# Scan steps of a gated encoder layer: masks in one instruction, the state's split at a step's beginning, an addition on GpSimd, and a gate's SiLU made in the attention

## The chip, the core and the metric

The kernel runs on one core of a Trainium2 chip. The time is the device time of one execution in microseconds, the median of three runs. The engines are TensorE (PE in the rows; PEld is its loading of weights), VectorE (DVE), ScalarE (ACT), GpSimd (POOL) and SyncE (SP), which only issues DMAs here.

## The reference

One encoder layer is applied to two sequences, of 512 and of 1024 tokens, each with a condition vector of its own; the width is 1024.

```python
h = rms_norm(x, norm_g) * (1 + scale) + shift          # shift, scale, gate from silu(c) @ w_ada + b_ada
proj = h @ w_in
(q_c, kv_c, k_rope, gate_a, z, xbc, dt_f_raw, dt_b_raw, g_a, g_b) = split(proj)
attn = mla_attention(q, k, v)                          # 8 heads; q, k, v from q_c, kv_c, k_rope
branch_a = (attn * silu(gate_a)) @ w_proj_a
xbc = silu(dwconv_centred(xbc, conv_w, conv_b))        # 5 taps
xs, B, C = split(xbc)
y = bidirectional_ssd(xs, dt_f, dt_b, A_f, A_b, B, C, d_f, d_b)
y = rms_norm(y * silu(z)) ; branch_b = y @ w_proj_b    # norm in 4 groups
out = x + gate * ((sigmoid(g_a) * branch_a + sigmoid(g_b) * branch_b) @ w_out)
```

The scan (`bidirectional_ssd`) works in chunks of 128 tokens, in 4 groups of 8 heads of 64 channels, with 128 state dimensions. In one direction, for a chunk with running sums `a` of the decays:

```python
CB     = C @ B.T                                       # 128 x 128, one for all heads of a group
y_diag = (CB * exp(where(tri, a_l - a_s, -inf))) @ (x * dt)
y_off  = (C @ state) * exp(a)                          # the part carried from other chunks
state  = state * exp(a_last) + B.T @ (exp(a_last - a) * dt * x)
```

The backward direction is the same on the reversed sequence, with the other triangle for a mask.

## The kernel before

All 1536 tokens are worked on in three windows of 512. A float32 product that has to be exact is made of three TensorE products (`mm3`, L88 to L90): a high part `h` (a rounded copy) and a low part `l` (the rest) of each factor. ACT makes the copy (L226 for weights, "wh<-ws"), DVE the rest (L85, "wl<-ws,wh").

The stages in order of time, in microseconds of the profile: a prologue (0 to 85); then four groups, each with its convolution blocks, its scan and its z gate; the attention (1598 to 2190); the final projections (2190 to 2714). The scans lie in the windows 219 to 386, 570 to 735, 937 to 1100 and 1330 to 1500.

**A scan.** `prepass` goes backwards through a sequence's chunks, makes the backward states and writes them to DRAM (sbD). `mainpass` goes forwards. The work of a chunk is cut into two units of four heads (`us`). For a chunk there are:

- `head` (L635): transposed blocks `xb` of x and B (for the first chunk of a sequence by `tok`, L588 to L592, on TensorE and ACT, otherwise loaded, L644), the product of B and C (L651, into PSUM "sm"), and its two masked copies `cu` (L653 and L654, DVE);
- `state` (L683): ACT copies (L688, L690) and GpSimd's subtractions (L689 "btl", L691 "zt") split the weighted x and B for the `mm3` of `follow` (L88 to L90 "sm<-zt,..."), after which DVE makes the new state (L607, L609 "stf");
- `decays` (L657): loads of the decays into `eb` (L663);
- `carried` (L667): an exponential on ACT (L672), the product of C and the carried state on TensorE (L677, into "sm"), its scaling (L678), and where both directions are there the sum of the two (L680, DVE).

And for a unit: `distances` (two loads `ab`, L706), `weights` (two subtractions on GpSimd, L714; eight scaled copies of `cu` on ACT, L718 and L719, and their sum on DVE, L720; a selection on DVE, L721; an exponential on ACT, L722), `weigh` (L727, DVE) and `products` (L738, TensorE, into PSUM "py"). `tail` (L743, L744, DVE) adds both parts up. PSUM has three slots "sm", which the transposes, the mask product, the state's product and the carried products use in turn.

Between a scan's steps `feed` puts pieces of other projections of the input, the fillers, at 0.66 of a piece for a step. One kind, "gate", is gate_a: from PSUM, ACT makes tanh of its half (L524), DVE makes (tanh + 1) times the gate (L525), and SP writes the result to DRAM (sgA, L526).

**The attention** works in 24 units (sequence, head, window). For each there is a list of work on the scores (`scores`: transposes, and four blocks with maxima and exponentials, L1025) and a list on the values (`values`). `merge` puts lists together in proportion, so that each entry's place depends on its list's length. The scores are one unit or more ahead of the values. `gates` makes the reciprocal sums `rb`, loads gate_a's part `gt` (L1042) and multiplies the two on GpSimd (L1043); at the end of a unit DVE multiplies the output by it and by 0.5 (L1072).

**Order.** Each engine works through a queue of its own in an order that is fixed when the program is built: a scheduler takes, by the order of the program and by what is ready in its own model, the next instruction for each engine. So where a line stands in the program moves instructions on every engine. Buffers (`bufs`) are used in turn; a second use waits for the last reader of the first.

Of the kernel before, what the change touches and what calls it, by code (L numbers as in the profile page):

```python
# [65 lines left out]
def _body(nc, tc, A, O):  # L66
# [447 lines left out]
    def filler(kind, i):  # L514
# [6 lines left out]
        elif kind == "gate":  # L521
            def ev(w, ps):
                t = tmp("ft")
                S.activation(t, ps, AF.Tanh, scale=0.5)  # L524
                V.scalar_tensor_tensor(t, t, 1.0, ps, op0=ALU.add, op1=ALU.mult)  # L525
                nc.sync.dma_start(out=sgA[i][w], in_=t)  # L526
            return inproj_steps(BLK_GATE + i, ev)
        else:
            dst = tga if kind == "ga" else tgb

            def ev(w, ps):
                t = tmp("ft")
                S.activation(t, ps, AF.Tanh, scale=0.5)
                nc.sync.dma_start(out=dst[i][w], in_=t)
            return inproj_steps((BLK_GA if kind == "ga" else BLK_GB) + i, ev)
# [34 lines left out]
    for g in range(G):  # L570
# [61 lines left out]
        def mainpass(o, n):  # L632
# [5 lines left out]
            def head(c):  # L638
# [8 lines left out]
                if c < c1 - 1:  # L647
                    sb = pS.tile([P, W], F32, name="sb", bufs=2)
                    nc.sync.dma_start(out=sb, in_=sbD[g][c])
                pc = smp.tile([P, P], F32, name="sm")  # L650
                PE.matmul(pc, lhsT=Bt[:, cs_], rhs=Ct[:, cs_], start=True, stop=True)  # L651
                cu = pS.tile([P, 2, P], F32, name="cu", bufs=2)
                V.tensor_tensor(cu[:, 0, :], pc, triF, op=ALU.mult)  # L653
                V.tensor_tensor(cu[:, 1, :], pc, triB, op=ALU.mult)  # L654
                stt[c] = dict(xt=xt, bt=bt, sb=sb, cu=cu)
# [11 lines left out]
            def carried(c):  # L667
# [11 lines left out]
                if len(eb) == 2:  # L679
                    V.tensor_tensor(eb[1], eb[1], eb[0], op=ALU.add)  # L680
# [66 lines left out]
            us = [(c, u) for c in range(c0, c1) for u in range(nu)]  # L747
            head(c0)
# [7 lines left out]
            for i in range(len(us) + 1):  # L756
                if i < len(us):
                    weigh(*us[i])
# [4 lines left out]
                if i < len(us) and us[i][1] == 1:  # L763
                    follow(us[i][0])
                    carried(us[i][0])
# [4 lines left out]
                if i < len(us) and us[i][1] == 0:  # L770
                    c = us[i][0]
                    state(c)
# [198 lines left out]
    def scores(u):  # L971
# [55 lines left out]

        def gates():
# [12 lines left out]
            gt = p2.tile([P, W], F32, name="gt", bufs=1)  # L1041
            nc.sync.dma_start(out=gt, in_=sgA[hd][o // W + w])  # L1042
# [4 lines left out]
        return [turn_n, turn_r], [lambda b=b: block(b) for b in range(4)]  # L1047
# [220 lines left out]
```

## Time and profile before

| | us |
|---|---|
| median of 3 runs | 2715.68 (2711.13 to 2715.99) |
| profiled execution, device time | 2716.42 |
| its span in the trace | 2714.4 |
| TensorE busy | 2586.5 (95%) |
| VectorE busy | 1833.5 (68%) |
| ScalarE busy | 1322.6 (49%) |
| GpSimd busy | 505.1 (19%) |

The mean granted clock of TensorE in the profiled execution was 0.985 of full speed. Busy time is a sum over stages with different limits; the shares of single stages, the waits of TensorE and single stretches in order of time are in the rows below. In a timeline row stand the start, the length, the engine, the line, the operation, the tiles "out<-in", the shape and, in brackets, how long the engine had been idle before it and what ended that.

### The profile page before, as it was taken

How to read it: one execution, taken by the hardware profiler on the slowest of the kernel's cores; microseconds unless marked ns; L12 is line 12 of the kernel's file. 1: busy time of each engine (PE TensorE's matmuls, PEld its weight loads, DVE VectorE, ACT ScalarE, POOL GpSimd, SP SyncE). 2: the span in 40 equal slices, each digit the busy share in tenths (PEclk: the TensorE clock that was granted, in tenths of full speed). 3: DMA queues.
4: the chain of work that ended last, by engine and by line, in shares of the span. 5: the costliest groups of instructions: out<-in, count | busy, mean ns of one | idle time of the engine just before them, and what ended most of it. 6: DMA issues, size and time to landing. Idle time of an engine off the chain costs nothing. (4 is left out here: it accounts for less than half of the span.)

```text
span 2714.4 us, 36314 instructions
## 1 busy us (share of the span) xinstructions
PE 2586.5 (95%) x12810; PEld 2080.5 (77%) x12810; DVE 1833.5 (68%) x2962; ACT 1322.6 (49%) x2954; POOL 505.1 (19%) x455
## 2 busy tenths in 40 slices
PE   6999999999999998999998999999999999999999
PEld 2776777877778766878766888888888788888887
DVE  5878785788946678557777568877777753466631
ACT  5545654456624456564556357666665651111210
POOL 1013440023400035110135024322222200000000
PEclk8999999999999999999999999999999999999999
DMA  7227662156722266542466322211110252255433
GB/s 249 77 78 208 187 168 94 39 179 187 207 62 86 82 208 183 136 147 74 146 191 188 92 96 87 84 44 43 34 40 28 71 186 70 78 156 163 128 125 101
DMA packets 211205, 325.86 MB, mean 120 GB/s; under 512 B 24816, under 2 KB 74064, under 8 KB 210256
## 3 DMA queue, kind: packets, MB, share of 16 engines
q1 hardware_dynamic: 211024, 323.55, 39.9%
q8 instruction: 101, 1.65, 0.3%
q14 instruction: 80, 0.66, 0.1%
HBM read 245.56 MB, written 77.91 MB: 119 GB/s over the span
## 5 line engine op out<-in xcount | busy, mean ns | idle before, releaser
L88 PE MATMUL mm<-hH,wh 128*128 128x512 f32 x1656 | 670.2, 405 | 2.3 <-ACT hH L218 2.0
L89 PE MATMUL mm<-hL,wh 128*128 128x512 f32 x1656 | 662.0, 400 | 3.6 <-DVE hL L219 3.6
L90 PE MATMUL mm<-hH,wl 128*128 128x512 f32 x1656 | 653.7, 395 | 1.3 <-DVE wl L85 1.2
L88 PEld LDWEIGHTS mm<-hH,wh 128*128 128x128 f32 x1656 | 314.6, 190 | 84.6 <-issue 14.6
L89 PEld LDWEIGHTS mm<-hL,wh 128*128 128x128 f32 x1656 | 315.4, 190 | 77.3 <-issue 10.2
L90 PEld LDWEIGHTS mm<-hH,wl 128*128 128x128 f32 x1656 | 314.6, 190 | 73.2 <-issue 6.1
L714 POOL TENSOR_TENSOR ab<-ab,dg 128x512 f32<-128x512 f32 x192 | 236.9, 1246 | 418.5 <-DMA ab<-arD 293.4
L88 PE MATMUL mm<-hi,wh 128*128 128x512 f32 x768 | 298.8, 389 | 0.0
L90 PE MATMUL mm<-hi,wl 128*128 128x512 f32 x768 | 298.8, 389 | 0.0
L89 PE MATMUL mm<-lo,wh 128*128 128x512 f32 x768 | 298.8, 389 | 0.0
L85 DVE TENSOR_TENSOR wl<-ws,wh 128x512 fp32r<-128x512 f32 x210 | 151.3, 722 | 134.4 <-ACT wh L226 86.7
L361 ACT CAST wh<-ws 128x512 fp32r<-128x512 f32 x72 | 44.9, 623 | 326.4 <-PE mm L89 311.3
L88 PEld LDWEIGHTS mm<-hi,wh 128*128 128x128 f32 x768 | 144.1, 188 | 30.1
L89 PEld LDWEIGHTS mm<-lo,wh 128*128 128x128 f32 x768 | 144.1, 188 | 29.9
L90 PEld LDWEIGHTS mm<-hi,wl 128*128 128x128 f32 x768 | 144.1, 188 | 29.9
L719 ACT ACTIVATE wt<-cu,dg 128x128 f32<-128x128 f32 x384 | 141.3, 391 | 46.5 <-DVE cu L653 46.1
L1025 ACT ACTIVATE pp<-sp,smx,rq 128x512 f32<-128x512 f32 x160 | 123.6, 777 | 54.9 <-DVE smx L1020 38.8
L361 ACT CAST ph<-tp 128x512 fp32r<-128x512 f32 x160 | 95.3, 598 | 110.4 <-PE tp L1059 110.2
L689 POOL TENSOR_TENSOR btl<-xb,bth 128x128 fp32r<-128x128 f32 x40 | 28.5, 713 | 607.5 <-ACT bth L688 607.4
L563 DVE SCALAR_TENSOR_TENSOR xs<-raw,cwh,xs 128x511 f32<-128x511 f32 (+3 forms) x128 | 129.7, 1021 | 17.5 <-ACT xs L559 14.8
L718 ACT ACTIVATE t<-cu,dg 128x128 f32<-128x128 f32 x384 | 137.3, 390 | 2.6 <-DVE cu L654 2.4
L721 DVE COPY_PREDICATED ab<-maskb,ab 128x512 f32<-128x512 uint8 x96 | 86.4, 905 | 69.3 <-POOL ab L714 69.3
(293 smaller groups left out, 5018.5 us busy)
## 6 DMA issues: line engine op xcount, KB each, us to landing
ab<-arD SPq DMA_DIRECT2D x192, 256.0 KB
ws<-w_in SPq DMA_DIRECT2D x140, 256.0 KB
eb<-arD SPq DMA_DIRECT2D x160, 128.0 KB
xbD<-xp SPq DMA_DIRECT2D x40, 320.0 KB
xb<-xbD SPq DMA_DIRECT2D x40, 320.0 KB
yT<-xs SPq DMA_DIRECT2D x48, 256.0 KB
sg<-yT SPq DMA_DIRECT2D x48, 256.0 KB
tg<-tga SPq DMA_DIRECT2D x48, 256.0 KB
```

Source lines behind the costliest of these rows:

```text
L85: V.tensor_tensor(out, a, b, op=ALU.subtract)
L88: PE.matmul(out, lhsT=ah, rhs=bh, start=first, stop=False)
L89: PE.matmul(out, lhsT=ah, rhs=bl, start=False, stop=False)
L90: PE.matmul(out, lhsT=al, rhs=bh, start=False, stop=last)
L361: S.copy(hi, src)
L563: V.scalar_tensor_tensor(acc[:, lo:hi], raw[:, lo + d:hi + d], cwh[:, 24 + 24 * k + tix:24 + 24 * k + tix + 1], acc[:, lo:hi], op0=ALU.mul ...
L689: GP.tensor_tensor(bl, stt[c]["bt"], r32(bh), op=ALU.subtract)
L714: GP.tensor_tensor(ab[:, d], ab[:, d], ac_[:, d, c, e0:e0 + HH].unsqueeze(2).broadcast_to([P, HH, P]), op=ALU.subtract)
L718: S.activation(t1[:, e], cu[:, 1, :], AF.Copy, scale=dt_[:, 1, c, e0 + e:e0 + e + 1])
L719: S.activation(wt[:, e], cu[:, 0, :], AF.Copy, scale=dt_[:, 0, c, e0 + e:e0 + e + 1])
L721: V.copy_predicated(ab[:, 0], maskb.unsqueeze(1).broadcast_to([P, HH, P]), ab[:, 1])
L1025: S.activation(pp[k], sps[k], AF.Exp, bias=sm[:, 2:3], scale=rq[:, b, h:h + 1], accum_out=st["su"][:, k, b:b + 1])
```

## The change

Four things are changed, which are separate in the code:

1. **Masks.** The mask product leaves `head` for a function `masks`. One DVE instruction multiplies the product, read twice, by the two triangles (columns 1 and 2 of `cmat`), 128x256, instead of two on 128x128. `masks(c0)` is called ahead of `head(c0)`, and `masks(c + 1)` at the beginning of chunk c's first unit.
2. **State's split.** `state(c)`, which was called near the end of a chunk's first unit, is called at its beginning, ahead of `weigh`.
3. **Sum of the carried parts.** The addition in `carried` goes from DVE to GpSimd.
4. **SiLU of gate_a.** The filler only copies the gate from PSUM (ACT) and writes it to DRAM. In the attention a fifth entry of a unit's list of scores, `silu`, loads it, makes the tanh on ACT and, on GpSimd, a product and a sum. The tile `gt` has three buffers instead of one, the tanh's tile one.

```diff
-                S.activation(t, ps, AF.Tanh, scale=0.5)
-                V.scalar_tensor_tensor(t, t, 1.0, ps, op0=ALU.add, op1=ALU.mult)
+                S.copy(t, ps)
                 nc.sync.dma_start(out=sgA[i][w], in_=t)
...
+                stt[c] = dict(xt=xt, bt=bt, sb=sb, cu=stt[c])
+
+            def masks(c):
+
+                cs_ = slice(c * P, (c + 1) * P)
                 pc = smp.tile([P, P], F32, name="sm")
                 PE.matmul(pc, lhsT=Bt[:, cs_], rhs=Ct[:, cs_], start=True, stop=True)
                 cu = pS.tile([P, 2, P], F32, name="cu", bufs=2)
-                V.tensor_tensor(cu[:, 0, :], pc, triF, op=ALU.mult)
-                V.tensor_tensor(cu[:, 1, :], pc, triB, op=ALU.mult)
-                stt[c] = dict(xt=xt, bt=bt, sb=sb, cu=cu)
+                V.tensor_tensor(cu, pc.unsqueeze(1).broadcast_to([P, 2, P]), cmat[:, 1:3, :], op=ALU.mult)
+                stt[c] = cu
...
                 if len(eb) == 2:
-                    V.tensor_tensor(eb[1], eb[1], eb[0], op=ALU.add)
+                    GP.tensor_tensor(eb[1], eb[1], eb[0], op=ALU.add)
...
+            masks(c0)
             head(c0)
...
             for i in range(len(us) + 1):
+                c, u = us[min(i, len(us) - 1)]
+                begins = i < len(us) and u == 0
+                if begins:
+                    if c + 1 < c1:
+                        masks(c + 1)
+                    state(c)
                 if i < len(us):
-                    weigh(*us[i])
+                    weigh(c, u)
...
-                if i < len(us) and us[i][1] == 0:
-                    c = us[i][0]
-                    state(c)
+                if begins:
                     decays(c)
                     if c + 1 < c1:
                         head(c + 1)
...
+        def silu():
+
+            gt = st["gt"] = p2.tile([P, W], F32, name="gt", bufs=3)
+            nc.sync.dma_start(out=gt, in_=sgA[hd][o // W + w])
+            tg = p2.tile([P, W], F32, name="tgt", bufs=1)
+            S.activation(tg, gt, AF.Tanh, scale=0.5)
+            GP.tensor_tensor(tg, tg, gt, op=ALU.mult)
+            GP.tensor_tensor(gt, tg, gt, op=ALU.add)
+
...
-            gt = p2.tile([P, W], F32, name="gt", bufs=1)
-            nc.sync.dma_start(out=gt, in_=sgA[hd][o // W + w])
+            gt = st["gt"]
             GP.tensor_tensor(gt, gt, rb, op=ALU.mult)
...
-        return [turn_n, turn_r], [lambda b=b: block(b) for b in range(4)]
+        return [turn_n, turn_r], [lambda b=b: block(b) for b in range(4)] + [silu]
```

What the change moves on the engines stands in the order of their instructions. In the rows that follow, line numbers of the kernel after differ by one to three from those before (L717 is L714 before, L724 is L721, L730 is L727, L746 and L747 are L743 and L744, L692 and L694 are L689 and L691, L608 is L609).

On DVE in the first group's scan (sequence 1, at 345 to 352 us of the trace before), the masks ("cu<-sm,cmat") before stand between the tail's two additions:

```order
L727 TENSOR_TENSOR wt<-ab,wt 128x512
L721 COPY_PREDICATED ab<-maskb,ab 128x512
L85 TENSOR_TENSOR wl<-ws,wh 128x512 x2
L525 SCALAR_TENSOR_TENSOR ft<-ft,mm 128x512
L743 TENSOR_TENSOR eb<-eb,py 128x512
L653 TENSOR_TENSOR cu<-sm,cmat 128x128
L744 TENSOR_TENSOR xs<-xs,eb 128x4x128
L654 TENSOR_TENSOR cu<-sm,cmat 128x128
```

The same place of the kernel after:

```order
L730 TENSOR_TENSOR wt<-ab,wt 128x512
L724 COPY_PREDICATED ab<-maskb,ab 128x512
L85 TENSOR_TENSOR wl<-ws,wh 128x512
L657 TENSOR_TENSOR cu<-sm,cmat 128x256
L746 TENSOR_TENSOR eb<-eb,py 128x512
L85 TENSOR_TENSOR wl<-ws,wh 128x512
L747 TENSOR_TENSOR xs<-xs,eb 128x4x128
```

The masks are one instruction now, and it moved ahead of the second L85, of the gate's product (which is gone) and of both of the tail's additions.

On GpSimd in the fourth group's scan (sequence 1, up to 1462 us of the trace before), the state's split (L689 and L691) before stands behind three subtractions of the units' distances (L714) and ahead of four:

```order
L691 TENSOR_TENSOR zt<-tmp,zt 128x512
L714 TENSOR_TENSOR ab<-ab,dg 128x512 x3
L689 TENSOR_TENSOR btl<-xb,bth 128x128
L691 TENSOR_TENSOR zt<-tmp,zt 128x512
L714 TENSOR_TENSOR ab<-ab,dg 128x512 x4
```

The same place of the kernel after:

```order
L717 TENSOR_TENSOR ab<-ab,dg 128x512 x2
L692 TENSOR_TENSOR btl<-xb,bth 128x128
L694 TENSOR_TENSOR zt<-tmp,zt 128x512
L717 TENSOR_TENSOR ab<-ab,dg 128x512
L683 TENSOR_TENSOR eb<-eb 128x512
L717 TENSOR_TENSOR ab<-ab,dg 128x512 x4
```

The split of a chunk moved ahead of the third subtraction, and the sum of the carried parts (L683) stands ahead of the four that follow.

On TensorE at the beginning of sequence 1's scan in the first group, the transposes (L588, L590) of its first chunk before stand ahead of the mask product (L651):

```order
L588 MATMUL sm<-cmat,xs 128x128 x4
L590 MATMUL sm<-cmat,kd 128x128
L651 MATMUL sm<-ch,kd 128x128
L88 MATMUL mm<-hH_401,wh 128x512
L89 MATMUL mm<-hL_404,wh 128x512
L90 MATMUL mm<-hH_401,wl 128x512
L88 MATMUL mm<-hH_401,wh 128x512
L651 MATMUL sm<-ch,kd 128x128
```

The same place of the kernel after (L655 is the mask product, L587 and L589 are the transposes):

```order
L655 MATMUL sm<-ch,kd 128x128
L587 MATMUL sm<-cmat,xs 128x128 x4
L589 MATMUL sm<-cmat,kd 128x128
L655 MATMUL sm<-ch,kd 128x128
L88 MATMUL mm<-hH_401,wh 128x512
```

The first chunk's mask product moved ahead of the transposes, and the second chunk's ahead of the filler's products that stood before it.

## Rows read from the trace of the kernel before

**Rows 1.** Windows by stage: us, busy us (count) of PE, PEld, DVE, ACT, POOL; PEclk, DMA share, GB/s.
```profile
219.00:386.00 167.00, 150.59 (x830) 116.02 (x829) 141.75 (x204) 103.23 (x282) 73.09 (x62) 0.96 0.72 200
570.00:735.00 165.00, 151.96 (x828) 117.28 (x827) 147.67 (x218) 107.99 (x297) 74.62 (x62) 0.98 0.72 204
937.00:1100.00 163.00, 144.38 (x751) 110.88 (x750) 123.42 (x183) 98.22 (x270) 65.68 (x56) 0.94 0.67 190
1330.00:1500.00 170.00, 152.97 (x821) 118.11 (x821) 133.59 (x200) 106.04 (x290) 74.17 (x61) 0.96 0.66 189
1598.00:2190.00 592.00, 567.33 (x3346) 491.26 (x3345) 452.49 (x995) 377.26 (x960) 165.53 (x168) 1.00 0.18 55
```

**Rows 2.** TensorE's waits: engine, line, releaser: us in total, times, longest us.
```profile
PE sm L677 <- DVE cu L654: 21.8, 7, 4.8
...
PE sm L89 <- POOL zt L691: 14.3, 10, 3.2
PE sm L626 <- DVE eb L678: 9.0, 4, 3.4
...
PE sm L651 <- ACT xb L592: 4.8, 3, 2.1
PE sm L590 <- DVE eb L678: 4.5, 5, 1.3
```

**Rows 3.** Timeline, 345 to 353 us, first group's scan.
```profile
347.35 0.67 DVE L85 TENSOR_TENSOR wl<-ws,wh 128x512 fp32r<-128x512 f32 x1
...
347.84 1.08 POOL L714 TENSOR_TENSOR ab<-ab,dg 128x512 f32<-128x512 f32 x1 [1.59 <-DMA ab<-arD]
...
348.65 0.82 DVE L85 TENSOR_TENSOR wl<-ws,wh 128x512 fp32r<-128x512 f32 x1 [0.63 <-ACT wh L226]
...
349.99 0.68 DVE L743 TENSOR_TENSOR eb<-eb,py 128x512 f32<-128x512 f32 x1
...
351.39 0.28 DVE L654 TENSOR_TENSOR cu<-sm,cmat 128x128 f32<-128x128 f32 x1
...
351.72 1.65 PE L677 MATMUL sm<-ch,sb 128*128 128x128 f32 x6 [4.31 <-DVE cu L654]
```

**Rows 4.** Windows around 706 us, columns as in rows 1.
```profile
701.00:706.00 5.00, 0.47 (x3) 0.03 (x1) 5.00 (x9) 2.73 (x6) 1.24 (x2) 1.00 0.49 154
706.00:710.00 4.00, 3.77 (x14) 3.34 (x15) 4.00 (x7) 4.00 (x15) 2.06 (x2) 0.57 0.96 258
```

**Rows 5.** Timeline, 1451 to 1465 us, fourth group's scan.
```profile
1451.72 3.79 POOL L714 TENSOR_TENSOR ab<-ab,dg 128x512 f32<-128x512 f32 x2 [6.62 <-DMA ab<-arD]
...
1455.88 1.72 POOL L691 TENSOR_TENSOR zt<-tmp,zt 128x512 fp32r<-128x512 f32 x1
...
1457.65 0.80 PE L89 MATMUL sm<-zt,bth 128*128 128x512 f32 x1 [3.10 <-POOL zt L691]
...
1460.07 0.73 DVE L721 COPY_PREDICATED ab<-maskb,ab 128x512 f32<-128x512 uint8 x1 [1.93 <-POOL ab L714]
...
1464.53 0.28 DVE L654 TENSOR_TENSOR cu<-sm,cmat 128x128 f32<-128x128 f32 x1
...
1464.87 0.58 PE L677 MATMUL sm<-ch,sb 128*128 128x128 f32 x1 [3.90 <-DVE cu L654]
```

**Rows 6.** Groups by line and form: count, busy us, mean ns, idle before and releasers.
```profile
L714 POOL TENSOR_TENSOR ab<-ab,dg 128x512 f32<-128x512 f32 x192 | 236.9, 1246 | 418.5 <-DMA ab<-arD 293.4 <-DMA arD<-cu 66.6 <-DVE eb L678 12.2
...
L1043 POOL TENSOR_TENSOR gt<-gt,rb 128x512 f32<-128x512 f32 x24 | 31.0, 1293 | 257.0 <-DMA rb<-rsD 217.0 <-DVE smx L1020 16.1 <-DVE qx L889 12.0
...
L824 ACT ACTIVATE zt<-xs 128x512 f32<-128x512 f32 x36 | 22.7, 631 | 47.8 <-DVE xs L822 44.6 <-DVE gate L286 3.1
...
L85 DVE TENSOR_TENSOR vl<-sp,vh 128x256 fp32r<-128x256 f32 x48 | 19.6, 414 | 0.1
```

**Rows 7.** Single lines: count; shortest/median/longest ns; first and last start; form.
```profile
L680 DVE TENSOR_TENSOR eb<-eb x32: 673/712/1778, 250.5 to 1498.8; 128x512 f32<-128x512 f32 x32
...
L743 DVE TENSOR_TENSOR eb<-eb,py x48: 668/676/689, 239.0 to 1508.2; 128x512 f32<-128x512 f32 x48
```

More of the change, by code (lines that the diff above doesn't have):

```diff
@@ L762, in mainpass @@
                     products(*us[i - 1])
-                if i < len(us) and us[i][1] == 1:
-                    follow(us[i][0])
-                    carried(us[i][0])
+                if i < len(us) and u == 1:
+                    follow(c)
+                    carried(c)
                 if i >= 1 and us[i - 1][1] == nu - 1:
```

## The prediction

> **What bounds the kernel now.** I read the stages first, in the windows [rows 1]: two numbers count, TensorE's busy time and PEclk, the granted share of its clock. In the four windows that hold a scan TensorE is busy 150.6 of 167, 152.0 of 165, 144.4 of 163 and 153.0 of 170 us: 65.1 us idle in 665. Its clock there is 0.96, 0.98, 0.94 and 0.96, which is 167 x 0.04 + 165 x 0.02 + 163 x 0.06 + 170 x 0.04 = 26.6 us' worth of clock withheld. In the attention (1598 to 2190) it is idle 24.7 us in 592 at 1.00. No TensorE work is added or removed by the change, so all that it can give back is idle time and withheld clock, and 92 us of the two lie in the scans.
>
> Next, TensorE's waits [rows 2], longest sum first: 21.8 us in 7 waits for the second mask (L654), 14.3 in 10 for GpSimd's half of the state's split (L691), 9.0 and 4.5 for the product L678, 4.8 in 3 for ACT's copy of a transposed block. That is 54.4 of the 65.1 us, and all but L691's are waits for one of three PSUM slots ("sm") that something has not yet read.
>
> Then two such waits in order of time. In [rows 3] TensorE stands 4.31 us until 351.72, since the slot of the mask product is read by L653 and L654, and these stand on DVE behind the second L85 (which itself waited 0.63 us for ACT), L525, L743 and L744. In [rows 5] it waits 3.10 us for L691, which ran behind two L714 (3.79 us), and 7 us later 3.90 us for the masks. [rows 4] shows what follows on such a wait: after 0.47 us of work in 5 us the granted clock of the next 4 us is 0.57, thus mostly at the lower of its two levels (1.2 instead of 2.4 GHz). A wait costs more than its length.
>
> **The change part by part.** The sum is made against the profiled execution, 2716.4 us, 0.7 above the median.
>
> *Masks and split, 36.1 us of waits [rows 2].* One mask instruction on 128x256 replaces two of 0.28 us. Nearest row: a DVE instruction of that size from PSUM takes 0.41 us [rows 6]; between 0.28 and 0.56, and I take 0.41. What counts is its place. At [rows 3] the order has it behind the next unit's L721 and the first L85, and ahead of L743, the second L85 and L744. So it no longer waits for the 3.4 us from the first L85's end (348.02) to L654's start. It now waits for L721, and that for the L714 of 347.84 to 348.92. If this L714 comes no earlier, the mask ends at 348.92 + 0.73 + 0.67 + 0.41 = 350.7 (L721's 0.73 from [rows 5]), 0.9 us before L654's end at 351.67; if it comes in time, at 348.02 + 0.73 + 0.41 = 349.2, 2.5 us before. SyncE's queue now has this L714's load ahead of the two loads of "eb", so I take 2.0 of 4.31 us, 46%. At [rows 5] the split moves ahead of one L714, but the mask wait that follows makes only the mask's end count. It comes behind L721 (to 1460.80) and one L85: 1460.80 + 0.67 + 0.41 = 1461.9 instead of 1464.81, 2.9 us earlier; the carried add, new on GpSimd ahead of the L714 pair that L721 needs, takes back up to 1.2: between 1.7 and 2.9. I take 2.2 of 7.0 us, 31%. The rest have one shape or the other; 38% of 36.1 us is **-13.7** (15% to 70%: -5 to -25).
>
> *The head, 4.8 us.* The masks' product stands ahead of the transposes in TensorE's order now, and its slot comes free with a mask of 0.41 us on DVE, not with ACT's copy of the block: **-4** (0 to -4.8).
>
> *The waits for L678, 13.5 us.* DVE loses 32 adds (L680, median 0.71 us [rows 7]), 24 products L525 (0.68 each, as L743, one input in PSUM too [rows 7]) and about 0.15 us in each of 48 masks: 23 + 16 + 7 = 46 us in all. At the begin of a scan the order also has L678 ahead of L607, one DVE instruction of this size. Three times 0.6 us, and 1 us for the lighter queue: **-2.8** (0 to -6).
>
> *The clock.* 20.5 of 65.1 us of idle time go, 31%; the same share of 26.6 us is **-8** (-2 if the waits that stay are those after which it falls, -24 if hardly one stays).
>
> *The add on GpSimd.* Bounds: the L714 row, same shape and engine, 1.25 us in the mean, so 32 x 1.25 = 40 us, against GpSimd's idle time of 90 us and more in each of these windows [rows 1]. The add stands in order: it waits for the second L678, and behind it stand L714 (then L721, the exponential, L727 and TensorE's products) and the split. Cover: before L714 GpSimd is idle 418.5 us, 293 of them waiting for a load [rows 6]. **+2** (0 if this idle time takes all, +15 if a third lands on TensorE).
>
> The two engines also hinder each other: the add (two inputs in SBUF) takes 673 ns at least and up to 1778 on DVE, while L743, of the same size with one input in PSUM, stays between 668 and 689 [rows 7].
>
> The Trainium skill's rule for this (SBUF — State Buffer, "Who interferes with whom"): a DVE instruction with two SBUF inputs and a GpSimd instruction that reads SBUF share one port pair, which the first one holds for its whole length. The spread of these two rows agrees with it. It speaks against this edit, since an add that leaves DVE can still hold DVE up: with it the sum is the -2 of the first rival below, without it the -25.5 that follows.
>
> *SiLU in the attention.* In the scan's fillers the tanh from PSUM becomes a copy from PSUM, at no change for ACT. In the attention ACT gets 24 tanh of about 0.63 us (as L824, an activation on the same shape from SBUF [rows 6]), 15 us on 377 busy of 592. GpSimd gets 48 x 1.29 (as L1043) = 62 us on 166. The 24 loads are the same, each asked for earlier, at a DMA share of 0.18 [rows 1]. Cover for the tanh is ACT's idle third, for the products GpSimd's idle 70%. L1043 and the key's scaling stand in the same queue; if they come late, TensorE waits for the output accumulator. The list that a unit's scores are merged from has 7 entries, not 6, so that its blocks move forward among the values: this may gain or lose. Nothing in the trace shows it, so its bounds are part of TensorE's 24.7 us of idle and the same again: **+1** (-4 to +10).
>
> Sum: -13.7 - 4 - 2.8 - 8 + 2 + 1 = -25.5, or 2690.9 on the profiled execution and **2690** on the median.
>
> **The rivals.** *Masks in the hands of GpSimd, no change (2714).* The masks now stand behind L721, which waits for L714, and ahead of that stands the add, which may hold DVE too. If each add costs DVE or this chain as much as left it (1.25 us against 0.71), terms one and three are nothing, the clock -1, and the sum is -4 - 1 + 2 + 1 = -2. For it: at [rows 3] L714 ended 0.9 us after DVE was ready for it. Against it: the load of that L714 is asked for earlier, and GpSimd is more than half idle.
>
> *The add's queue, slower (2731).* If three quarters of the 32 adds push L714, and with it the products on TensorE, by their whole 1.25 us, that is 30 us of new waits and, at 26.6 us of clock for 65.1 of idle, 12 more: 2716.4 - 27.5 + 42 = 2731. It ends on the slower side once more than about half of the adds land so (27.5 / (40 x 1.41) = 0.49). Against it speak the 293 us that L714 waits for loads, where an add costs nothing; for it, places as in [rows 5], where two L714 run back to back for 3.79 us.
>
> *Much faster (2655).* Were two thirds of the 65.1 us to go and nearly all of the clock: 2716.4 - 43 - 22 + 3 = 2654. For it: at [rows 5] the wait for the masks follows the wait for the split by 7 us, so that one early split may move a whole step forward. Against it: L721 and its loads stay where they are.
>
> **How the numbers follow.** Forecast 62%, its own range 2672 to 2706 from the terms' ends taken half; no change 14%; slower 11%; much faster 13%. The range of 8 in 10 leaves out the slower case and half of the much faster one: 2664 to 2714. A run of this kernel can tell 0.2%, 5.4 us, from nothing; faster by more than that are the forecast and the much faster case, 75%, within it 14%, slower 11%.
>
> **What would show it.** Right: TensorE's waits for the mask instruction under 15 us in sum and for the split under 8; no long wait of a product into "sm" for ACT's copy; PEclk in the scan windows up by 0.01 to 0.02; TensorE's idle time in the attention within 5 us of 24.7. Wrong: waits that name the add or L714 as their releaser (the slower rival), a mask instruction that starts as late after its product as L654 did (no change), or ACT's tanh waiting for a load with the casts of the weights queued behind it.

## The result and the profile after

The changed kernel is slower: 2757.27 us (2753.32 to 2760.56, 4 runs) against 2715.84 (2711.13 to 2720.78), a ratio of 1.0149, interval 1.0133 to 1.0165. The profiled execution has a span of 2755.8 us, 41.4 more than before; the mean granted clock fell from 0.985 to 0.977.

The stages come later now, so that the windows of [rows 1] do not hold the same work any more. I took each scan from its first transpose to the last addition of its tail, and the attention from its first transpose to the last product with the gate. The windows of the kernel before by these bounds (us, then busy us and count of PE, PEld, DVE, ACT, POOL, then PEclk, DMA share, GB/s):

```profile
196.80:394.40 197.60, 181.09 (x968) 139.33 (x966) 162.01 (x232) 117.99 (x316) 80.18 (x69) 0.97 0.69 195
554.40:750.90 196.50, 183.46 (x986) 141.48 (x985) 169.29 (x244) 119.35 (x318) 82.05 (x68) 0.98 0.69 198
923.30:1126.70 203.40, 184.77 (x974) 142.29 (x973) 154.26 (x224) 118.93 (x317) 73.97 (x62) 0.95 0.66 188
1309.90:1509.30 199.40, 182.37 (x973) 140.51 (x972) 152.85 (x229) 118.90 (x316) 74.63 (x62) 0.97 0.63 186
1609.70:2188.90 579.20, 556.69 (x3284) 481.41 (x3283) 446.59 (x976) 370.57 (x939) 162.22 (x164) 1.00 0.18 54
```

and of the kernel after:

```profile
194.90:407.20 212.30, 183.43 (x951) 141.91 (x950) 153.74 (x205) 118.44 (x316) 88.89 (x77) 0.93 0.63 182
571.30:782.90 211.60, 189.16 (x1004) 146.30 (x1002) 150.67 (x206) 119.44 (x318) 89.20 (x76) 0.96 0.64 184
952.20:1160.60 208.40, 186.99 (x980) 144.95 (x980) 148.48 (x204) 119.11 (x317) 84.05 (x70) 0.94 0.65 184
1341.10:1552.60 211.50, 189.59 (x982) 146.96 (x982) 150.94 (x209) 118.79 (x317) 80.07 (x70) 0.93 0.61 175
1651.00:2230.30 579.30, 562.57 (x3283) 485.27 (x3282) 456.32 (x982) 385.57 (x970) 222.59 (x211) 0.99 0.17 54
```

The attention is as long as it was (579.2 and 579.3 us), with 60 us more of GpSimd's work in it. The whole loss lies in the scans: 796.9 us before, 843.8 after. Of these 46.9 us, 29.4 are idle time of TensorE (65.2 to 94.6 us), and 17.5 are longer busy time at a lower clock (3917 products are recorded in these windows, 3901 before, so a little of it may be work that fell into them). DVE is busy 34.6 us less in them (638.4 to 603.8), as the change meant it to be; so DVE's load did not set their length.

TensorE's waits after (columns as in [rows 2]: line, releaser, us in total, times, longest):

```profile
PE sm L680 <- DVE cu L657: 27.4, 7, 8.2
...
PE sm L625 <- DVE raw L608: 14.0, 4, 4.6
PE py L741 <- DVE wt L730: 11.4, 6, 4.1
PE mm L90 <- DVE wl L85: 10.5, 8, 2.4
PE sm L625 <- DVE eb L681: 9.3, 5, 2.4
PE sm L655 <- DVE stf L608: 9.3, 9, 2.7
```

The waits for the split (L89, 14.3 us before, 0.4 after) and for ACT's copy (4.8) are gone, as forecast. The wait for the masks (L680 <- L657) is still the longest and has grown from 21.8 to 27.4 us, and four waits, all for DVE, are new or larger by 7 us or more: those at L625 for L608 (none before), at L741 (2.9 before), at L90 (1.2) and at L655 (1.9). What DVE waits for in turn (before, only the first of these two stood there, with 69.3 us in 39 waits):

```profile
DVE ab L724 <- POOL ab L717: 88.3, 43, 4.6
...
DVE eb L746 <- POOL eb L683: 47.9, 12, 5.8
```

One such wait in order of time, first on GpSimd, then on DVE, then on TensorE (the kernel after, 246 to 255 us):

```profile
246.07 1.59 POOL L717 TENSOR_TENSOR ab<-ab,dg 128x512 f32<-128x512 f32 x1 [7.56 <-PE sm L589]
247.63 0.90 POOL L692 TENSOR_TENSOR btl<-xb,bth 128x128 fp32r<-128x128 f32 x1
248.49 3.02 POOL L717 TENSOR_TENSOR ab<-ab,dg 128x512 f32<-128x512 f32 x3
251.49 1.25 POOL L683 TENSOR_TENSOR eb<-eb 128x512 f32<-128x512 f32 x1
```
```profile
246.68 1.53 DVE L597 TENSOR_TENSOR tmp<-xp,dg 128x512 f32<-128x512 f32 x1
252.77 0.69 DVE L746 TENSOR_TENSOR eb<-eb,py 128x512 f32<-128x512 f32 x1 [4.56 <-POOL eb L683]
253.38 0.68 DVE L608 TENSOR_TENSOR raw<-raw,sm 128x512 f32<-128x512 f32 x1
```
```profile
254.11 2.07 PE L625 MATMUL sm<-tmp,xp 128*128 128x512 f32 x2 [4.57 <-DVE raw L608]
```

The sum (L683) had its inputs at 246.16 (the end of L681), but runs behind the distances. DVE stands 4.56 us at the tail, L746, and behind it stands L608, which would free TensorE's slot. This made my first theory: the sum costs by DVE's wait for it. It fell (e17 below).

### The profile page after: what moved, and what is told of

It is laid out like the page before. It is cut to its first block, busy times and chain, and to the rows that moved or that the text cites. A ratio compares the mean times of both kernels' runs of the same rounds, so it can differ in the third digit from the quotient of the medians.

```text
span 2755.8 us, 36381 instructions
## 1 busy us (share of the span) xinstructions
PE 2604.3 (95%) x12810; PEld 2097.3 (76%) x12810; DVE 1807.6 (66%) x2858; ACT 1336.2 (48%) x2978; POOL 599.5 (22%) x535
## 4 chain that ended last, share of the span: by engine, by line
PE 54%; DVE 5%; DMA 5%; ACT 3%; POOL 3%; issue 2%; SPq 0%; POOLq 0%; ACTq 0%; DVEq 0%
PE mm L88 12%; PE mm L90 12%; PE mm L89 12%; PE tp L1075 2%; DMA ab<-arD 2%; PE sp L90 1%; PE sp L89 1%; PE sp L88 1%; PE sp L1020 1%; PE sp L1021 1%; PE sp L1024 1%; PE sp L1022 1%; PE sp L1023 1%; PE po L88 1%; POOL ab L717 1%
## 5 line engine op out<-in xcount | busy, mean ns | idle before, releaser
L90 PE MATMUL mm<-hH,wl 128*128 128x512 f32 x1656 | 665.6, 402 | 10.5 <-DVE wl L85 10.5
L89 PE MATMUL mm<-hL,wh 128*128 128x512 f32 x1656 | 661.4, 399 | 2.0 <-DVE hL L219 2.0
L90 PEld LDWEIGHTS mm<-hH,wl 128*128 128x128 f32 x1656 | 318.4, 192 | 87.9 <-DVE wl L85 15.2
L89 PEld LDWEIGHTS mm<-hL,wh 128*128 128x128 f32 x1656 | 318.0, 192 | 75.7 <-issue 7.9
L717 POOL TENSOR_TENSOR ab<-ab,dg 128x512 f32<-128x512 f32 x192 | 228.0, 1197 | 420.4 <-DMA ab<-arD 304.9
L89 PE MATMUL mm<-lo,wh 128*128 128x512 f32 x768 | 298.8, 389 | 0.0
L90 PE MATMUL mm<-hi,wl 128*128 128x512 f32 x768 | 298.8, 389 | 0.0
L85 DVE TENSOR_TENSOR wl<-ws,wh 128x512 fp32r<-128x512 f32 x210 | 153.7, 734 | 135.7 <-ACT wh L226 86.8
L90 PEld LDWEIGHTS mm<-hi,wl 128*128 128x128 f32 x768 | 144.1, 188 | 29.9
L89 PEld LDWEIGHTS mm<-lo,wh 128*128 128x128 f32 x768 | 144.1, 188 | 29.8
L692 POOL TENSOR_TENSOR btl<-xb,bth 128x128 fp32r<-128x128 f32 x40 | 28.5, 714 | 615.0 <-ACT bth L691 614.9
L721 ACT ACTIVATE t<-cu,dg 128x128 f32<-128x128 f32 x384 | 145.6, 393 | 23.6 <-DVE cu L657 23.6
L724 DVE COPY_PREDICATED ab<-maskb,ab 128x512 f32<-128x512 uint8 x96 | 95.3, 996 | 88.3 <-POOL ab L717 88.3
L562 DVE SCALAR_TENSOR_TENSOR xs<-raw,cwh,xs 128x511 f32<-128x511 f32 (+3 forms) x128 | 130.5, 1027 | 17.5 <-ACT xs L558 14.9
L1025 DVE TENSOR_REDUCE smx<-sp 128x1 f32<-128x512 f32 x160 | 108.0, 685 | 37.7 <-PE sp L1024 37.2
```

The lines of the kernel that those rows point to most:

```text
L85: V.tensor_tensor(out, a, b, op=ALU.subtract)
L89: PE.matmul(out, lhsT=ah, rhs=bl, start=False, stop=False)
L90: PE.matmul(out, lhsT=al, rhs=bh, start=False, stop=last)
L562: V.scalar_tensor_tensor(acc[:, lo:hi], raw[:, lo + d:hi + d], cwh[:, 24 + 24 * k + tix:24 + 24 * k + tix + 1], acc[:, lo:hi], op0=ALU.mul ...
L717: GP.tensor_tensor(ab[:, d], ab[:, d], ac_[:, d, c, e0:e0 + HH].unsqueeze(2).broadcast_to([P, HH, P]), op=ALU.subtract)
L721: S.activation(t1[:, e], cu[:, 1, :], AF.Copy, scale=dt_[:, 1, c, e0 + e:e0 + e + 1])
```

## The experiments

All ratios are to the kernel before on the same chip, with 95% intervals. Line numbers in a row are those of the kernel that it is from.

| run | what it has of the change | ratio | interval |
|---|---|---|---|
| after | all | 1.0149 | 1.0133 to 1.0165 |
| e1 | all but the sum on GpSimd | 1.0062 | 1.0045 to 1.0079 |
| e2 | the sum on GpSimd | 1.0138 | 1.0114 to 1.0161 |
| e3 | masks and split | 1.0038 | 1.0025 to 1.0052 |
| e4 | SiLU | 1.0026 | 1.0016 to 1.0037 |
| e5 | masks | 0.9987 | 0.9973 to 1.0002 |
| e6 | split | 1.0050 | 1.0032 to 1.0068 |
| e7 | a quarter of the sum on GpSimd, the rest of it left out | 1.0065 | 1.0048 to 1.0083 |
| e8 | no sum at all | 1.0045 | 1.0030 to 1.0061 |
| e9 | SiLU, the fillers' half (the attention's is left out) | 1.0022 | 1.0010 to 1.0034 |
| e10 | SiLU, the attention's half (made twice) | 1.0002 | 0.9986 to 1.0017 |
| e11 | e3 with xb's load first | 1.0012 | 0.9999 to 1.0025 |
| e12 | e5 with xb's load first | 0.9996 | 0.9977 to 1.0015 |
| e13 | e2 with a third buffer | 1.0207 | 1.0187 to 1.0226 |
| e14 | before with the buffers of e13 | 1.0048 | 1.0032 to 1.0064 |
| e15 | all, with xb's load first | 1.0156 | 1.0141 to 1.0171 |
| e16 | sum on DVE, at the tail | 0.9994 | 0.9979 to 1.0009 |
| e17 | no sum; in its place an addition on GpSimd that nothing reads | 1.0128 | 1.0108 to 1.0148 |
| e18 | e5, mask product later | 1.0014 | 1.0001 to 1.0026 |

### Which part costs (e1 to e4)

e1, to the kernel after:

```diff
-                    GP.tensor_tensor(eb[1], eb[1], eb[0], op=ALU.add)
+                    V.tensor_tensor(eb[1], eb[1], eb[0], op=ALU.add)
```

> The changed kernel with the sum of the carried parts back on DVE; masks, split and SiLU stay as changed. Theory A (the sum's place in GpSimd's queue: in the changed kernel's trace DVE stood 47.9 us in 12 waits at the tail's first addition, L746, until GpSimd's sum, L683, behind which the next masks and states then came late): that wait is gone and the time is below the kernel before, 2690 to 2712, ratio 0.991 to 0.999. Rival B (masks and split, moved ahead, now stand behind the selection L724 that waits for GpSimd's distances): the time stays at 2740 to 2757, ratio 1.009 to 1.015. Rival C (the SiLU): likewise unchanged, 2745 or more.

e2, to the kernel before:

```diff
-                    V.tensor_tensor(eb[1], eb[1], eb[0], op=ALU.add)
+                    GP.tensor_tensor(eb[1], eb[1], eb[0], op=ALU.add)
```

> The kernel before with only the sum of the carried parts moved to GpSimd. Theory A: most of the loss, 2740 to 2765, ratio 1.009 to 1.018, and DVE waits for the sum at L743 by 40 us or more in all. Rivals B and C: no loss, 2710 to 2722.

e3 and e4 are the kernel before with the diff's parts 1 and 2, and with its part 4.

> The kernel before with only the mask instruction and the split moved, sum on DVE, SiLU in the fillers. Theory A: faster than before, 2695 to 2712, TensorE's waits for the mask under 15 us. Rival B: slower, 2740 or more, with waits for the mask of 20 us and more. Rival C: 2710 to 2722.

> The kernel before with only the SiLU moved to the attention. Theory A and rival B: within 6 us of the kernel before (2710 to 2722), the attention's idle time of TensorE within 5 us of 24.7. Rival C: 2740 or more.

Measured: 1.0062, 1.0138, 1.0038, 1.0026. The sum is the largest part, as theory A said, but A was wrong on the rest: without the sum the change is still slower. Masks with split, and the SiLU, each lose, and e1 has just their product (1.0038 x 1.0026 = 1.0064). The sum costs 0.9% on top of them (1.0149 / 1.0062 = 1.0086) and 1.4% alone.

One link of this can be seen between e1 and the kernel after, which differ by the sum alone. TensorE's waits for the masks are 27.4 us after, and half of that in e1:

```profile
PE sm L655 <- DVE stf L608: 25.4, 7, 7.7
...
PE sm L680 <- DVE cu L657: 13.7, 7, 4.3
```

The same place as in [rows 3], in the kernel after: GpSimd, then DVE, then TensorE.

```profile
351.29 1.26 POOL L683 TENSOR_TENSOR eb<-eb 128x512 f32<-128x512 f32 x1
352.51 2.94 POOL L717 TENSOR_TENSOR ab<-ab,dg 128x512 f32<-128x512 f32 x2
```
```profile
355.48 0.73 DVE L724 COPY_PREDICATED ab<-maskb,ab 128x512 f32<-128x512 uint8 x1 [0.93 <-POOL ab L717]
...
356.70 0.42 DVE L657 TENSOR_TENSOR cu<-sm,cmat 128x256 f32<-128x256 f32 x1
```
```profile
357.18 1.22 PE L680 MATMUL sm<-ch,sb 128*128 128x128 f32 x4 [5.37 <-DVE cu L657]
```

The sum stands ahead of the two distances that the selection L724 waits for, and the masks, moved ahead, now stand behind that selection. This is the chain of the rival "masks in the hands of GpSimd". It is not the whole cost: the waits for the state's slot (L655 <- L608) go the other way, from 25.4 us in e1 to 9.3. Over the whole kernel TensorE is idle 12.6 us longer than in e1 (151.5 against 138.9) and busy 13.9 us longer.

In e3 the waits that were to go did go: for the masks 10.6 us in place of 21.8, for the split 0.2 in place of 14.3. But TensorE's longest wait there is a new one, at the mask product:

```profile
PE sm L656 <- DVE stf L609: 29.9, 7, 7.2
...
PE sm L681 <- DVE cu L658: 10.6, 8, 2.7
```

The longest of them, 7.20 us, in order of time: SyncE's queue, then DVE, then TensorE (e3, 1092 to 1104 us; L656 is the mask product, L598 the weighting that begins the split):

```profile
1092.29 4.94 SPq L667 DMA_DIRECT2D eb<-arD  x3
1097.32 0.55 SPq L644 DMA_DIRECT2D xb<-xbD  x1
```
```profile
1096.60 0.69 DVE L731 TENSOR_TENSOR wt<-ab,wt 128x512 f32<-128x512 f32 x1
1102.10 0.69 DVE L598 TENSOR_TENSOR tmp<-xb,dg 128x512 f32<-128x512 f32 x1 [4.81 <-DMA xb<-xbD]
1102.71 0.68 DVE L609 TENSOR_TENSOR stf<-stf,sm 128x512 f32<-128x512 f32 x1
```
```profile
1103.44 0.79 PE L656 MATMUL sm<-ch,kd 128*128 128x128 f32 x2 [7.20 <-DVE stf L609]
```

The load of xb was issued behind the loads of eb. The split, moved ahead, has DVE at a block that is not there yet; the state's addition L609 stands behind it and holds a PSUM slot; the next mask product, also moved ahead, needs that slot; and behind it stands all of TensorE's queue.

### Masks against split (e5, e6)

e5, to e3, puts `state(c)` back where it was:

```diff
                     if c + 1 < c1:
                         masks(c + 1)
-                    state(c)
...
                 if begins:
+                    state(c)
                     decays(c)
```

e6, to the kernel before:

```diff
+                if i < len(us) and us[i][1] == 0:
+                    state(us[i][0])
                 if i < len(us):
                     weigh(*us[i])
...
                     c = us[i][0]
-                    state(c)
                     decays(c)
```

> The kernel before with only the masks changed: one instruction, product ahead at the chunk's beginning; the split stays where it was. With masks and split together (ratio 1.0038) TensorE waited 29.9 us in 7 waits at the mask product for a PSUM slot that DVE's state addition L609 had not freed. Theory P (the mask product, now ahead in TensorE's queue, needs a slot earlier than DVE frees one): slower, ratio 1.003 to 1.010, with 20 us or more of such waits. Theory X (the split, now ahead, makes DVE wait for the load of xb, and the state addition stands behind it): this part alone is faster, ratio 0.992 to 0.998, such waits under 8 us.

> The kernel before with only the state's split moved to the chunk's beginning. Theory P: faster or unchanged, ratio 0.994 to 1.001, since the waits for GpSimd's split (14.3 us before) go. Theory X: slower, ratio 1.003 to 1.010, with DVE waiting for the load of xb at L598 by 3 us and more in several places.

Measured 0.9987 and 1.0050: the loss is the split's. The masks alone gain at most a little (the interval reaches 1.0002), and not the 0.2 to 0.8% that theory X expected; the mask product still waits 18.2 us for a slot in e5 (e18 below tries what that is worth). In e6 DVE waits 14.3 us for xb at L598, more than the 6.2 us before.

### Fillers against attention (e9, e10)

e9 is the kernel before with the first hunk of the change's diff alone:

```diff
-                S.activation(t, ps, AF.Tanh, scale=0.5)
-                V.scalar_tensor_tensor(t, t, 1.0, ps, op0=ALU.add, op1=ALU.mult)
+                S.copy(t, ps)
```

e10 is the kernel before with the rest of part 4 (`silu` in the list of scores, `gt` from it).

> The kernel before with only the fillers' half of the SiLU change: the gate is copied from PSUM and written as it is; the attention is as before and takes it so (the SiLU is left out). With the whole SiLU change (ratio 1.0026) the attention took as long as before (578.4 against 579.2 us), and the loss lay ahead of it. If the loss comes from the scans' changed order, though DVE has 24 products less: ratio 1.001 to 1.005. If it comes from the attention's new work: 0.996 to 1.000.

> The kernel before with only the attention's half of the SiLU change: tanh, product and sum there, the fillers as before (so that SiLU is made twice). If the loss comes from the scans: within 0.1% of the kernel before, ratio 0.999 to 1.001. If from the attention's work on ACT and GpSimd: 1.002 to 1.005.

Measured 1.0022 and 1.0002: the SiLU's loss comes from the fillers, although DVE has 24 instructions less there; TensorE's waits for the masks are 25.5 us in e9 (21.8 before) and those for the split 17.4 (14.3). The attention takes its new work, 24 tanh and 48 products and sums, at nothing that could be measured.

### The split's load (e11, e12, e15)

To e3, e5 and the kernel after:

```diff
-                    decays(c)
                     if c + 1 < c1:
                         head(c + 1)
+                    decays(c)
```

> Masks and split as changed, sum on DVE, SiLU in the fillers (ratio 1.0038 so far), and the loads of the next chunk's xb and sb put ahead of the loads of eb in SyncE's queue. Theory X (the split now ahead on DVE waits for xb, whose load stood behind up to 4.9 us of waiting in that queue): the waits of L598 for xb go and the time falls by 8 us or more, ratio 0.996 to 1.001. If the split's place on the engines costs by itself: the ratio stays at 1.003 to 1.005.

> Only the masks as changed (ratio 0.9987 so far), and the same swap of loads. The split is not ahead here, so that theory X expects no gain of it: ratio 0.996 to 1.001. A ratio over 1.002 would say that the later load of eb costs as much as the earlier one of xb gives.

> The whole change, with the loads of the next chunk's xb and sb ahead of those of eb. If the split's cost by late loads adds to the sum's: ratio 1.010 to 1.013 in place of 1.0149. If the sum's waits cover it: 1.014 to 1.016.

Measured 1.0012 for e11 against 1.0038 for e3; the kernel with masks alone does not change by it (0.9996 and 0.9987). DVE's waits for xb at L598 in e3 and in e11:

```profile
DVE tmp L598 <- DMA xb<-xbD: 14.0, 5, 4.8
```
```profile
DVE tmp L598 <- DMA xb<-xbD: 6.1, 6, 2.2
```

and TensorE's waits at the mask product fell with them, from 29.9 to 15.5 us. So most of the split's cost is the late load, as theory X says; nothing is gained by it even so. In the whole change the same swap gives nothing (e15, 1.0156), and there was little to give: DVE waits only 7.3 us for xb in the kernel after, and 7.5 in e15.

### What of the sum costs (e7, e8, e13, e14, e16, e17)

e7, to the kernel before (e8 drops these lines):

```diff
                 if len(eb) == 2:
-                    V.tensor_tensor(eb[1], eb[1], eb[0], op=ALU.add)
+                    GP.tensor_tensor(eb[1][:, 0:1], eb[1][:, 0:1], eb[0][:, 0:1], op=ALU.add)
```

> The kernel before with the sum of the carried parts on GpSimd, over a quarter of its columns only (the rest of the sum is left out). If the sum costs by its place in GpSimd's queue (behind the distances, and SyncE's queue waiting for it before it may load the next decays): most of the loss of 37 us stays, ratio 1.008 to 1.014. If it costs by its length on GpSimd (1.29 us each): a quarter of it stays, ratio 1.001 to 1.005.

> The kernel before without the sum of the carried parts (it is left out, one of the two parts is taken). What DVE's relief of 32 additions is worth by itself. If TensorE's waits go with DVE's load, as the prediction had it: 2.8 us or more less with clock, ratio 0.990 to 0.998. If they go by the order and by loads: 0.998 to 1.002.

Measured 1.0065, between the two ranges expected for e7, and 1.0045, above both of those for e8. Taking 32 additions from DVE, with nothing in their place, makes the kernel slower by 0.45%. A quarter of the sum on GpSimd adds 0.2% to that, which the two intervals don't tell from nothing, and the full sum 0.9%: the sum's length on GpSimd counts (medians 0.62 and 1.29 us), and less so its place, which is about the same in e2 and e7.

Where e8's time goes I can show at one place. After the loss of the sum the order on DVE has the selection (L719, L721 before) ahead of the tail's second addition (L742). DVE and SyncE, e8:

```profile
1001.81 0.68 DVE L741 TENSOR_TENSOR eb<-eb,py 128x512 f32<-128x512 f32 x1
1005.84 1.56 DVE L719 COPY_PREDICATED ab<-maskb,ab 128x512 f32<-128x512 uint8 x1 [3.35 <-POOL ab L712]
1007.29 1.51 DVE L742 TENSOR_TENSOR xs<-xs,eb 128x512 f32<-128x512 f32 x1
```
```profile
1008.83 0.58 SPq L663 DMA_DIRECT2D eb<-arD  x1
```

The tail's end frees a buffer of eb. Before, its two additions ran in one piece at 1002.85 to 1004.26, and the load went out at 1004.29; here it goes out at 1008.83. ACT's exponential of eb then waits for loads, with the copy of the transposed block behind it, and TensorE waits 5.41 us for that copy, not 2.05. Over the whole kernel ACT's waits for loads of eb are 83.3 us in e8 and 52.3 before. That this is the whole of the 0.45% is not shown. Order alone need not cost: e16 moves the sum on DVE to the tail,

```diff
-                if len(eb) == 2:
-                    V.tensor_tensor(eb[1], eb[1], eb[0], op=ALU.add)
...
+                if len(eb) == 2:
+                    V.tensor_tensor(eb[1], eb[1], eb[0], op=ALU.add)
                 V.tensor_tensor(off, off, stt[c]["py"], op=ALU.add)
```

> The kernel before with the same sum on the same engine, DVE, but written at the tail, right ahead of its first addition, in place of after the scalings. No instruction is added, taken away or moved to another engine. If the loss without any sum (e8) is one of the order: this too moves the time by 0.3% or more, either way. If it isn't: within 0.2%.

and that changes nothing (0.9994). So a changed order on DVE need not cost, and that e8's loss comes from its own order is not shown beyond this one place.

e13, to e2 (e14 is the same to the kernel before; a third place, where the same buffers of eb are used by later work, gets the same count):

```diff
-                    eb[d] = pS.tile([P, 4, P], F32, name="eb", bufs=2)
+                    eb[d] = pS.tile([P, 4, P], F32, name="eb", bufs=3)
...
-                t1 = pS.tile([P, HH, P], F32, name="t1", bufs=2)
+                t1 = pS.tile([P, HH, P], F32, name="t1", bufs=1)
```

> The kernel before with the sum on GpSimd, eb with three buffers in place of two, and t1 with one in place of two to make room. Theory D (late buffers): against its control e14 a ratio of 1.000 to 1.005, and SyncE's waits for the sum ahead of loads of eb, 120.6 us with two buffers, under 40. Theory Q (waits in order on DVE and GpSimd): against the control still 1.008 to 1.014, and DVE's waits for the sum at L743 (24.3 us) and for the distances at L721 (90.2) stay.

> The control: the kernel before with eb in three buffers and t1 in one. All theories: 0.990 to 1.010 of the kernel before; it is what e13 is compared with.

Measured 1.0207 and 1.0048, thus 1.0158 for the sum: no gain from the third buffer. The test is weaker than meant, since SyncE's waits for the sum only fell from 120.6 to 102.9 us; theory D expected under 40.

e17, to the kernel before:

```diff
-                    V.tensor_tensor(eb[1], eb[1], eb[0], op=ALU.add)
+                    GP.tensor_tensor(eb[0], eb[0], eb[0], op=ALU.add)
```

> The kernel before with an addition of the same size in the same place on GpSimd that reads and writes the first part of eb alone, which nothing reads afterwards; the tail takes the other part (the sum is left out, as in e8, ratio 1.0045). GpSimd is as long at work and the first buffer comes free as late as with the sum on GpSimd, but DVE's tail doesn't wait for it. If DVE's wait at the tail is the cost (24.3 us in 12 waits): ratio 1.003 to 1.007. If GpSimd's time and the late buffers are: 1.010 to 1.015.

Measured 1.0128, against 1.0138 with the sum that DVE waits for. DVE's waits for the sum at the tail (24.3 us in e2) are gone and the time is the same. So the wait that looked like the cause in the trace is not the cost: where DVE doesn't wait for the sum, it waits at the same instruction for TensorE's products (L743 <- L738, 17.7 us, 2.6 in e2). SyncE's loads of eb do wait for the addition in e17 too, 88.5 us in 29 waits (120.6 in e2). What e2 and e17 also share, and before has not, are longer waits for what GpSimd does behind the sum. TensorE's waits for the split in e2 and in e17 (14.3 us in [rows 2]):

```profile
PE sm L89 <- POOL zt L691: 21.8, 10, 5.0
```
```profile
PE sm L89 <- POOL zt L691: 22.3, 13, 5.0
```

and one of them, GpSimd in e2 at 349 to 354 us, where the sum stands between a distance and the split, for which TensorE waits 4.95 us, until 353.94:

```profile
349.41 1.13 POOL L714 TENSOR_TENSOR ab<-ab,dg 128x512 f32<-128x512 f32 x1 [0.92 <-DMA ab<-arD]
350.50 1.70 POOL L680 TENSOR_TENSOR eb<-eb 128x512 f32<-128x512 f32 x1
352.17 1.71 POOL L691 TENSOR_TENSOR zt<-tmp,zt 128x512 fp32r<-128x512 f32 x1
```

These waits are not the cost by themselves. In e13 they are only 10.6 us, and the sum costs as much there; e18 below has 22.5 us of them at 1.0014. The same holds for SyncE's waits for the sum: e7 has 96.3 us of them, at 0.2% over e8. TensorE's idle time, 25.9 us longer in e2 than before (153.8 against 127.9), is spread over several waits: 7.5 us more for the split, 7.6 for the low parts of weights (L90 <- L85), 6.5 for the state's addition at the transposes (L588 <- L609), 6.4 for ACT's copy (L651 <- L592).

### The mask product's slot (e18)

e18, to e5:

```diff
-                if begins:
-                    if c + 1 < c1:
-                        masks(c + 1)
                 if i < len(us):
                     weigh(c, u)
...
                 if i >= 1:
                     products(*us[i - 1])
+                if begins and c + 1 < c1:
+                    masks(c + 1)
```

> Only the masks as changed (ratio 0.9987), but the next chunk's mask product stands behind the products of the unit before, instead of ahead of weigh. If the mask product's waits for a PSUM slot (18.2 us in 7 waits at L656 behind L609) hold the masks' gain back: these waits under 12 us and a ratio of 0.993 to 0.997. If not: 0.998 to 1.001.

Measured 1.0014. The waits for the slot fell as meant, from 18.2 to 6.6 us, but those for the split grew to 22.5 (10.3 in e5). A wait that goes is again replaced by the next one in the same chain. No version here is clearly faster than the kernel before.

## Why the prediction was wrong

*What bounds the kernel.* Right that the scans' idle time and clock decide and that the attention doesn't. Wrong that the waits in the table of [rows 2] are a sum from which parts can be taken: each names the last link of a chain through four engines and SyncE's queue, and in e3, e17 and e18 the wait named went and another came.

*Masks and split, -13.7: the step that failed with the sign.* The order was read only for what the masks and the split now stand ahead of. What they now wait for was not priced: the split begins with DVE's weighting of xb, whose load SyncE issues behind eb's, and the mask product needs a PSUM slot earlier. Measured: masks 0.9987 (about -4 us), split 1.0050 (about +14), both 1.0038 (+10). The forecast for the mask's end by [rows 3] was made for one place with the rest held still.

*The head, -4.* The waits of the mask product for ACT's copy are gone from the list after (4.8 us in [rows 2]): right so far. But the same product now waits 9.3 us for the state's addition (L655 <- L608; 1.9 before), so that the 4 us were not gained.

*The waits for L678, -2.8.* 13.5 us before, 11.1 after (9.3 at L625 and 1.8 at L589): the size is near. Of the two causes given, DVE's lighter load is not borne out: e8 with 32 additions less has 11.5 us of these waits, e9 with 24 products less 14.7, e3, which keeps both on DVE, 9.1; and e8 and e9 are slower. The other, the order at a scan's beginning, was not tried alone. At L625 itself 14.0 us of waits for L608 came in addition.

*The clock, -8.* It followed the idle time, as assumed, the other way: 0.985 to 0.977. In the scans TensorE's busy time grew by 17.5 us beside 29.4 us of idle time. After the wait of 5.37 us for the masks shown under e1, TensorE's clock in the kernel after (columns as above) is 0.50, so at the lower level of 1.2 GHz:

```profile
350.00:357.00 7.00, 1.80 (x13) 1.48 (x11) 5.14 (x6) 1.83 (x4) 5.45 (x4) 0.87 0.60 165
357.00:362.00 5.00, 4.83 (x15) 4.19 (x16) 4.23 (x7) 4.67 (x14) 2.54 (x2) 0.50 0.96 284
```

*The add on GpSimd, +2: the largest miss.* It measured 1.0086 x 2716 less 2716, about 23 us, in the whole change and 37 alone, beyond the bound of +15. The step that failed is the cover: 418.5 us in which GpSimd stood idle ahead of L714, 293.4 of them for loads [rows 6]. That was taken for slack. In e2 GpSimd has 48 us of sums to make, and the idle time ahead of L714 hardly shrinks:

```profile
L714 POOL TENSOR_TENSOR ab<-ab,dg 128x512 f32<-128x512 f32 x192 | 232.0, 1218 | 400.2 <-DMA ab<-arD 300.7 <-DMA arD<-cu 66.7 <-DVE wt L720 7.9
```

SyncE's loads are issued in order, and those of eb wait for the sum (120.6 us in e2; before, 21.0 us for the same sum on DVE). GpSimd also stands 39.6 us ahead of the sum in e2, until DVE's scaling L678 is done; the prediction names this wait and gives it no price. And 169 of the 418.5 us lie outside the four scans (67.6 ahead of the first, 101.4 between the third and the fourth), where there is no sum to cover. So the idle time could not be counted as room. The slower rival, with 11%, had the signs right (waits that name the add and L714) and the mechanism at most in part: in e2 the products' waits are 3.0 us, 2.9 before. Its size, 42 us of loss less 27.5 of gain, was wrong in both parts.

*Contention on the ports.* The selection, which reads its mask and both parts of ab from SBUF, takes 996 ns in the mean after and 905 before, while the tail's first addition (L746), with one input in PSUM, keeps its 680 (678 before).

```profile
L721 DVE COPY_PREDICATED ab<-maskb,ab 128x512 f32<-128x512 uint8 x96 | 86.4, 905 | 69.3 <-POOL ab L714 69.3
```
```profile
L724 DVE COPY_PREDICATED ab<-maskb,ab 128x512 f32<-128x512 uint8 x96 | 95.3, 996 | 88.3 <-POOL ab L717 88.3
```

The Trainium skill (SBUF — State Buffer, "Who interferes with whom") has a DVE instruction with two SBUF inputs contend with a GpSimd instruction that reads SBUF; these two rows agree. Other instructions of this kind became shorter (L747 from 823 to 788 ns, L606 on the state from 842 to 749). Over all lines of this kind in the scan (selection, L723, L730, L747, L597, L606) DVE's busy time grows by 4.3 us, from 412.3 to 416.6, so that longer instructions on DVE alone don't make up the sum's 23 us. The rival "no change" was not what happened, though its other half, the masks behind GpSimd's distances and the sum, can be seen under e1.

*SiLU in the attention, +1.* Right for the attention (e10, 1.0002). The half that had been costed at nothing, the fillers' copy, is what costs (e9, 1.0022, 6 us): the prediction had it at no change for ACT and the 24 products that leave DVE as a gain. Why it is a loss the runs don't show.

**What stays open.** By which of its links the sum's time on GpSimd reaches TensorE (the split behind it, the distances, or the loads of eb) is not separated: e17 excludes DVE's wait for the sum at the tail, e13 speaks against the buffers without deciding, and the waits for the split and for the sum's buffer come without such a loss in e18 and e7. Why a kernel without the sum is slower (e8) is shown at one place only, and for the fillers (e9) not at all: in both the order of all engines changed, and that this is the reason is not shown.

## What to carry to other kernels

An engine that is idle 80% of the time may still be inside the loop that sets the step: before work is moved to it, follow what stands behind the new instruction in that engine's queue, and which loads wait for the buffer that it frees. Moving an instruction ahead needs both lists, what it no longer stands behind and what it will now wait for, its operands' loads and its PSUM slot too, since all that follows in the queue waits with it. And a wait in a table is worth its length only if nothing in the same chain is late next: try each part of a change alone, for here the split removed the waits it was meant to remove and lost time, and so did the sum and the fillers' copy, which took work off DVE.

## What the runs showed that I had not expected

Taking work away from DVE, which was busy 82 and 86% of the time in the first two scans, made the kernel slower twice (e8, 32 additions, 1.0045; e9, 24 products, 1.0022). And an addition whose result nothing reads (e17), though loads wait for its buffer, cost as much as one that DVE waits for.
